# Another order of the head pairs in a hybrid decoder step: 1, 2, 3, 0 for the delta rule and 1, 0 for retention and GLA

## The chip, the cores and the metric

The kernel is one program on one core of a Trainium2 chip. The core has a matrix engine (TensorE, PE in the profile; its weight loads are PEld), a vector engine (VectorE, DVE), a scalar engine (ScalarE, ACT), GpSimd (POOL) and a queue engine, SyncE (SP), that issues most of the transfers between the chip's DRAM and its on-chip memory. The metric is the device time of one execution in microseconds (us); lower is better.

## The reference

One layer of a decoder is computed for 256 prompt tokens and for 8 x 4 sample tokens, 288 columns in all, which share the weights. The three mixers read the same normalised input, each through its own columns of one wide weight matrix, and their outputs are merged:

```python
h = rmsnorm(x, norm_mix)
(rq, rk, rv, rg, dqkv, da, db, dz, lq, lk, lv, llr, lgt, mg) = jnp.split(h @ w_in, IN_OFFSETS, axis=-1)
# branch 0: retention, 4 heads (dk 128, dv 256), gated by silu(rg)
# branch 1: gated delta rule, 8 heads (dk = dv = 128), conv of width 4 over q, k, v, gated by silu(dz)
# branch 2: GLA, 4 heads (dk 128, dv 256), a forget gate from llr, gated by silu(lgt)
br = jnp.einsum('blnc,ncd->blnd', jnp.stack([y_ret, y_gdn, y_gla], axis=2), w_branch)
gates = jax.nn.sigmoid(mg + b_merge).reshape(b, l, 3, D_MODEL)
x = x + jnp.sum(gates * br, axis=2) @ w_o
x = x + swiglu(rmsnorm(x, norm_ffn))      # w_gate_up, w_down
```

All numbers are float32, D_MODEL is 2048, and the width of the feed-forward part is 5632. Besides the two outputs y, the new recurrent states of all heads and the last rows before the convolution are written. The heads of a mixer do not depend on each other.

## The kernel before

The activations are held transposed, 16 blocks of 128 rows by 288 columns, each split into a high and a low part (`xh`, `xl`). A weight block goes through the same steps everywhere: SyncE loads it (`raw`, a ring of 4 buffers of 512 KB), ScalarE copies the high part (`wh`, lines 353, 384, 420), VectorE subtracts for the low part (`wl`, line 133), and TensorE does three matmuls, high by high, high by low, low by high (line 127).

The mixers work by pairs of heads: 4 pairs of the delta rule (`gdn`), 2 of retention (`ret`), 2 of GLA (`gla`). A pair's dense part is projections: a delta-rule pair takes four of 256 columns (`gdn_conv` for query, key and value, and `gated` for the gate dz), a pair of the other two takes two of 256 (query, key) and two of 512 (value, gate, in `two_heads`). Each projection of 256 columns is 4 loads of 512 KB, each of 512 columns 8.

The rest of a pair (scores, states, norms) is a generator that is started when its projections are done and is advanced a step at a time by `pump`, called between the matmuls of the projections that follow. So a pair's own work runs beside the projections of the pairs behind it. The order is written out in `run`: delta rule 0, retention 0, delta rule 1, retention 1, delta rule 2, GLA 0, delta rule 3, GLA 1. When all delta-rule generators have ended, `branch(0, 0)` starts, the projection of retention's output; the last GLA pair is advanced within it. Then come `branch(1, 1)` for the delta rule, `branch(2, 2)` for GLA, `merge_out` and `ffn`.

Three things pass from one stage to another through DRAM:

- `ys`, 3 x 8 blocks of 128 x 288: each head stores its output (`finish`, line 647; one block for a delta-rule head, block h for head h; two for the others, blocks 2h and 2h + 1), and `branch` loads the eight blocks of its mixer in the order 0 to 7 into two buffers `yr` (line 1317) and splits them into `yh` and `yl`;
- `fsum`, the running sums of GLA's forget gates for both pairs, stored by `gate_cols` (line 548) and loaded by `gla` (line 1299);
- small scratch of the delta rule's triangular solve, whose place does not depend on the pair.

The first pair has three things of its own. In `setup`, the loads of its query weights are issued ahead, in halves of 256 KB between the loads of the input (line 209), and their products are made while the input is still being prepared (`self.early`, line 255). In `gdn`, the small projections for decay, beta and GLA's low-rank gate (`gates`, lines 446 to 474) stand between its key and its value. In `run`, constants of the wide heads are loaded (`wide_setup`) ahead of the first retention pair.

Code that depends on a head's number takes a column of a constant (`gcol`, `elb`, `sel`, `ccols`, `qdec`, `c_decay`, conv weights), a slice of a state in DRAM, a decay factor as an immediate, and the parity `h % 2` for one of two buffers.

The order of instructions on each engine is set before the run by a planner (`TileContext` with `schedule_with_timeline_sim=True`): it takes them by their place in the program, with the loads and splits of weights at a higher priority, as their dependencies, buffers and engines come free in its own model, and puts in the semaphore waits.

Of the kernel before, what the change touches and what calls it, by code (L numbers as in the profile page):

```python
# [25 lines left out]
KT = D // P  # L26
# [5 lines left out]
CHUNK = 256  # L32
# [7 lines left out]
R1 = 4  # L40
R2 = 6
EV = 9

O_RQ, O_RK, O_RV, O_RG = 0, 512, 1024, 2048
O_GQ, O_GK, O_GV = 3072, 4096, 5120
# [50 lines left out]
def blocks(t):  # L96
    return [t[:, k] for k in range(t.shape[1])]


class Trunk:  # L100
# [74 lines left out]
    def setup(self):  # L175
        nc, tc = self.nc, self.tc
# [23 lines left out]
        for n in range(D // XC):  # L200
            cs = slice(n * XC, (n + 1) * XC)
            nc.sync.dma_start(out=xa[:, :, cs], in_=xv[:, :, cs])  # L202
            if n == 0:
                nc.sync.dma_start(out=xb, in_=self.i["x_sample"].rearrange("b t c -> (b t) c"))
            if n % 2 == 0:
                raw = self.t(self.wp, (P, 4, CHUNK), "raw", bufs=4)
                self.ahead.append(raw)
            ks = slice(2 * (n % 2), 2 * (n % 2) + 2)
            nc.sync.dma_start(out=raw[:, ks], in_=self.w_in(O_GQ)[:, 2 * n:2 * n + 2])
        xd = self.t(self.dr, (KT, P, T), "xT")  # L210
        self.xT = xd
        self.ys = self.t(self.dr, (3, 8, P, T), "ys")
# [21 lines left out]
        def prep():  # L234
            for n in range(D // XC):
                xr = self.t(x0, (P, 2, T), "xr", bufs=4)
                for q in range(2):
                    k = 2 * n + q
                    ks = slice(k * P, (k + 1) * P)
                    pt = self.ps()  # L240
                    for g, (t0, w) in enumerate(GROUPS):
                        self.tr(pt[:, t0:t0 + w], xa[:, g, ks] if g < 2 else xb[:, ks])
                    gc = self.g_mix[:, k:k + 1]
                    self.act(self.xh[:, k, :], pt[:, :T], AF.Copy, scale=gc)
                    self.stt(self.xl[:, k, :], pt[:, :T], gc, self.xh[:, k, :].bitcast(F32), ALU.mult, ALU.subtract)
                    (nc.vector.tensor_copy if q else nc.scalar.copy)(xr[:, q], pt[:, :T])
                nc.gpsimd.dma_start(out=xd[2 * n:2 * n + 2].rearrange("k p t -> p k t"), in_=xr)
                yield
            while True:
                yield  # L250

        steps = prep()
        for _ in range(2):
            next(steps)
        self.early = self.products(blocks(self.xh), blocks(self.xl), self.w_in(O_GQ), KT, False, steps, False)
        ra = self.t(x0, (112, P), "ra")
        rows(nc.gpsimd, "norm_ffn", ra[96:112])
        nc.gpsimd.dma_start(out=ra[0:96], in_=self.i["gdn_conv_w"][0].rearrange("w (b p) -> (w b) p", p=P))
# [293 lines left out]
    def gdn_conv(self, pair, part):  # L552
# [8 lines left out]
        smp = [cat[:, mm_, 3 + NPR:CW].rearrange("p (b r) -> p b r", r=7) for mm_ in range(2)]  # L561
        out = self.t(m, (P, 2, T), "ev", bufs=EV)

# [40 lines left out]
    def gated(self, n, c0):  # L604

        out = self.t(self.mx, (P, 2, T), "ev", bufs=EV)

# [9 lines left out]
    def two_heads(self, cv, cg, head, kind):  # L617

        vs = [self.t(self.mx, (P, 2, T), "ev", bufs=EV) for _ in range(2)]

# [5 lines left out]
        self.start(head(0, vs[0], gates), 1, kind)  # L626
        gs = [self.t(self.mx, (P, 2, T), "ev", bufs=EV) for _ in range(2)]

# [349 lines left out]
    def gdn(self, pair):  # L978
        q = self.gdn_conv(pair, 0)
        k = self.gdn_conv(pair, 1)  # L980
        if pair == 0:
            self.gates()
        v = self.gdn_conv(pair, 2)
        sz = self.gated(2, O_DZ + pair * CHUNK)
        self.start(self.gdn_mix(pair, q, k, v, sz), 1, "gdn")
# [111 lines left out]
    def evict_scaled(self, c0, perm=False):  # L1097
        out = self.t(self.mx, (P, 2, T), "ev", bufs=EV)

        def ev(m, pp):  # L1100
            self.tt(out[:, m], pp, self.rb, ALU.mult)

        self.x_in(c0, ev, perm)
        return out


    def rotated(self, c0):
        out = self.t(self.mx, (P, 2, T), "ev", bufs=EV)

        def ev(m, pp):  # L1110
            b = self.r1()
            self.tt(b[0:64], pp[64:128], self.rot[64:128, 1], ALU.mult)
            self.tt(b[64:128], pp[0:64], self.rot[0:64, 1], ALU.mult)
            self.tt(out[:, m], pp, self.rot[:, 0], ALU.mult)
            self.tt(out[:, m], out[:, m], b, ALU.add)

        self.x_in(c0, ev, perm=True)
        return out
# [350 lines left out]
    def run(self):  # L1469
        self.setup()  # L1470
        mst, gst, fst, bst = (ExitStack() for _ in range(4))
        dst = ExitStack()
        self.mx = self.pool("mixers", stack=mst, side="right")
        self.wd = self.pool("wide", stack=mst, side="right")
        self.gd = self.pool("gdn", stack=dst, side="right")
        self.gdn_setup()
        for f, pair in ((self.gdn, 0), (self.ret, 0), (self.gdn, 1), (self.ret, 1),
                        (self.gdn, 2), (self.gla, 0), (self.gdn, 3), (self.gla, 1)):
            if f == self.ret and pair == 0:
                self.wide_setup()  # L1480
            f(pair)
        while any(kind == "gdn" for _, _, kind in self.active):
            self.pump()
        dst.close()
        self.bp = self.pool("branch", stack=bst)
        self.branch(0, 0)
        while self.active:
            self.pump()
        mst.close()
        self.ap = self.pool("accum", side="right")  # L1490
        self.acc = self.accs()
        self.branch(1, 1)
        mp = self.pool("merged", stack=gst, side="right")
        mt = [self.t(mp, (P, KT, T), f"m{z}", F32R) for z in range(2)]
        merged = [(mt[0][:, k], mt[1][:, k]) for k in range(KT)]

        def emit(k, a):
            hi, lo = merged[k]
            self.act(hi, a, AF.Copy, scale=0.5)
            self.stt(lo, a, 0.5, hi.bitcast(F32), ALU.mult, ALU.subtract)  # L1500

        self.branch(2, 2, emit=emit)
        self.merge_out(merged, mp)
        gst.close()
        bst.close()
        self.actp = self.pool("act")
        self.ffn(fst)
        fst.close()
# [38 lines left out]
```

## Time and profile before

| | |
|---|---|
| timed runs, us | 2267.48, 2272.69, 2272.87 (median 2272.69) |
| profiled execution, us | 2270.85 |
| its span, first to last instruction, us | 2269.0 |
| mean granted TensorE clock | 0.978 of full speed |
| TensorE busy, us | 2178.8 (96%) |
| VectorE busy, us | 1356.2 (60%) |
| ScalarE busy, us | 1026.6 (45%) |
| GpSimd busy, us | 204.9 (9%) |
| read from DRAM, written to it | 342.02 MB, 26.92 MB |

The span is what the profile's rows divide up; the execution's own time is 1.85 us longer. Busy times are shares of that span. The granted clock is what the throttle gave TensorE, 1.00 being 2.4 GHz and 0.5 being 1.2 GHz; a stretch between the two has parts at either.

### The profile page before, as it was taken

The numbers are of one execution on the slowest core, as the hardware profiler recorded it, in microseconds if no ns is written. First come the engines' busy times: TensorE is split into PE (matmuls) and PEld (weight loads), VectorE is DVE, ScalarE is ACT, GpSimd is POOL, SyncE is SP. The second block draws the span as 40 slices with busy tenths as digits, with TensorE's granted clock in tenths as the row PEclk, the third lists the DMA queues.
The fourth block names the chain that finished last, engine by engine and source line by source line (L and its number), as shares of the span: only waits on it lengthen the run. The fifth ranks groups of instructions, "written<-read, shape, count | busy, mean of one in ns | idle before, by whom it ended". The sixth has DMA issues, their size and how long they took to land.

```text
span 2269.0 us, 42856 instructions
## 1 busy us (share of the span) xinstructions
PE 2178.8 (96%) x16476; PEld 2117.5 (93%) x16476; DVE 1356.2 (60%) x2940; ACT 1026.6 (45%) x2114; POOL 204.9 (9%) x264
## 2 busy tenths in 40 slices
PE   8699998998999999999999999999999999999997
PEld 7688898998898999999999999999999999999997
DVE  4465686686589577555556566555655445555554
ACT  4353553454355345444444455444444334444443
POOL 2000320232143124000000000000000000000000
PEclk8799999998999999999999999999999999999999
DMA  9876675587567555766666556655555555555553
GB/s 176 107 127 141 134 192 151 135 164 167 118 154 197 154 157 178 213 190 176 189 185 167 165 179 184 184 164 165 166 168 167 167 162 167 166 167 168 167 159 117
DMA packets 258456, 371.73 MB, mean 164 GB/s; under 512 B 26242, under 2 KB 126684, under 8 KB 258092
## 3 DMA queue, kind: packets, MB, share of 16 engines
q1 hardware_dynamic: 257084, 366.22, 61.6%
q8 instruction: 129, 2.11, 0.4%
q0 software_dynamic: 896, 2.45, 0.3%
q14 instruction: 75, 0.61, 0.1%
q10 hardware_dynamic: 272, 0.34, 0.1%
HBM read 342.02 MB, written 26.92 MB: 163 GB/s over the span
## 4 chain that ended last, share of the span: by engine, by line
PE 79%; DMA 11%; DVE 4%; ACT 2%; SPq 1%; issue 1%; POOL 1%; POOLq 0%; DVEq 0%; ACTq 0%
PE pd L127 48%; PE pm L127 30%; DMA raw<-in_w_in_dram 4%; DMA yr<-ys 2%; DVE wl L133 1%; DMA s<-in_state_ret_dram 1%; PE pm L124 1%; DMA srow<-in_state_gdn_conv_dram 1%; DMA out_dram<-s 1%; DMA dgu<-u 1%; DVE r L142 1%; DMA uc<-dgu 0%; DMA ys<-yo 0%; SPq L202 0%; ACT wh L420 0%
## 5 line engine op out<-in xcount | busy, mean ns | idle before, releaser
L133 DVE TENSOR_TENSOR wl<-raw,wh 128x512 fp32r<-128x512 f32 (+1 forms) x1208 | 847.8, 705 | 727.4 <-ACT wh L384 490.9
L127 PE MATMUL pd<-xh,wh 128*128 128x288 f32 x2768 | 831.3, 302 | 21.9 <-ACT wh L420 14.3
L127 PE MATMUL pd<-xl,wh 128*128 128x288 f32 x2768 | 832.0, 301 | 0.2 <-DVE xl L142 0.2
L127 PE MATMUL pd<-xh,wl 128*128 128x288 f32 x2768 | 824.4, 302 | 2.2 <-DVE wl L133 2.0
L384 ACT CAST wh<-raw 128x512 fp32r<-128x512 f32 x784 | 485.1, 620 | 644.6 <-PE pd L127 333.6
L127 PEld LDWEIGHTS pd<-xh,wh 128*128 128x128 f32 x2768 | 529.6, 192 | 29.3 <-ACT wh L420 15.8
L127 PEld LDWEIGHTS pd<-xh,wl 128*128 128x128 f32 x2768 | 527.0, 192 | 8.5 <-DVE wl L133 5.6
L127 PEld LDWEIGHTS pd<-xl,wh 128*128 128x128 f32 x2768 | 530.8, 192 | 3.9 <-issue 1.2
L353 ACT CAST wh<-raw 128x512 fp32r<-128x512 f32 x224 | 137.7, 619 | 206.0 <-PE pd L127 187.7
L127 PE MATMUL pm<-xh,wl 128*128 128x288 f32 x704 | 207.8, 295 | 0.0
L127 PE MATMUL pm<-xl,wh 128*128 128x288 f32 x704 | 207.3, 294 | 0.0
L127 PE MATMUL pm<-xh,wh 128*128 128x288 f32 x704 | 207.0, 294 | 0.0
L420 ACT CAST wh<-raw 128x512 fp32r<-128x512 f32 x192 | 117.3, 620 | 116.5 <-DMA raw<-in_w_in_dram 54.8
L127 PEld LDWEIGHTS pm<-xl,wh 128*128 128x128 f32 x704 | 132.1, 188 | 0.0
L127 PEld LDWEIGHTS pm<-xh,wh 128*128 128x128 f32 x704 | 132.1, 188 | 0.0
L127 PEld LDWEIGHTS pm<-xh,wl 128*128 128x128 f32 x704 | 132.0, 188 | 0.0
L127 PE MATMUL pd<-ah,wl 128*128 128x288 f32 x352 | 103.9, 295 | 0.0
L127 PE MATMUL pm<-ah,wl 128*128 128x288 f32 x352 | 103.9, 295 | 0.0
L127 PE MATMUL pm<-al,wh 128*128 128x288 f32 x352 | 103.8, 295 | 0.0
L127 PE MATMUL pd<-al,wh 128*128 128x288 f32 x352 | 103.7, 295 | 0.0
L127 PE MATMUL pm<-ah,wh 128*128 128x288 f32 x352 | 103.7, 295 | 0.0
L127 PE MATMUL pd<-ah,wh 128*128 128x288 f32 x352 | 103.6, 294 | 0.0
(368 smaller groups left out, 2892.0 us busy)
## 6 DMA issues: line engine op xcount, KB each, us to landing
raw<-in_w_in_dram SPq DMA_DIRECT2D x252, 512.0 KB
raw<-in_w_gate_up_dram SPq DMA_DIRECT2D x176, 512.0 KB
raw<-in_w_down_dram SPq DMA_DIRECT2D x88, 512.0 KB
raw<-in_w_branch_dram SPq DMA_DIRECT2D x48, 512.0 KB
raw<-in_w_o_dram SPq DMA_DIRECT2D x32, 512.0 KB
out_dram<-s SPq DMA_DIRECT2D x16, 512.0 KB
s<-in_state_gdn_dram SPq DMA_DIRECT2D x8, 512.0 KB
s<-in_state_ret_dram SPq DMA_DIRECT2D x16, 256.0 KB
```

Of the source, the lines that this page charges most:

```text
L124: self.nc.tensor.transpose(out, in_, self.ident[:k, :k])
L127: self.nc.tensor.matmul(out, lhsT=lhsT, rhs=rhs, start=start, stop=stop)
L133: self.nc.vector.tensor_tensor(out, a, b, op=op)
L142: self.nc.vector.scalar_tensor_tensor(out, a, s, b, op0=op0, op1=op1)
L353: nc.scalar.copy(wh, src)
L384: nc.scalar.copy(wh, raw[:, k])
L420: nc.scalar.copy(h, src)
```

## The change

The order of the pairs becomes a constant, `ORDER = (1, 2, 3, 0)`, for the delta rule, and 1, 0 for retention and for GLA. The kinds still alternate as before: delta rule 1, retention 1, delta rule 2, retention 0, delta rule 3, GLA 1, delta rule 0, GLA 0. What belongs to the first delta-rule pair (loads ahead, early products, the gates' place) follows the pair that is first.

```diff
+ORDER = (1, 2, 3, 0)
...
-            nc.sync.dma_start(out=raw[:, ks], in_=self.w_in(O_GQ)[:, 2 * n:2 * n + 2])
+            nc.sync.dma_start(out=raw[:, ks], in_=self.w_in(O_GQ + ORDER[0] * CHUNK)[:, 2 * n:2 * n + 2])
...
-        self.early = self.products(blocks(self.xh), blocks(self.xl), self.w_in(O_GQ), KT, False, steps, False)
+        self.early = self.products(blocks(self.xh), blocks(self.xl), self.w_in(O_GQ + ORDER[0] * CHUNK), KT, False, steps, False)
...
         k = self.gdn_conv(pair, 1)
-        if pair == 0:
+        if pair == ORDER[0]:
             self.gates()
...
-        for f, pair in ((self.gdn, 0), (self.ret, 0), (self.gdn, 1), (self.ret, 1),
-                        (self.gdn, 2), (self.gla, 0), (self.gdn, 3), (self.gla, 1)):
-            if f == self.ret and pair == 0:
+        for n, (f, pair) in enumerate(((self.ret, 1), (self.ret, 0), (self.gla, 1), (self.gla, 0))):
+            self.gdn(ORDER[n])
+            if n == 0:
                 self.wide_setup()
             f(pair)
```

## Rows read from the trace of the kernel before

**Rows 1.** The profile page, head and part 1: busy us, share, instructions.

```profile
span 2269.0 us, 42856 instructions
...
PE 2178.8 (96%) x16476; PEld 2117.5 (93%) x16476; DVE 1356.2 (60%) x2940; ACT 1026.6 (45%) x2114; POOL 204.9 (9%) x264
```

**Rows 2.** The profile page, part 4: the chain that ended last, by engine.

```profile
PE 79%; DMA 11%; DVE 4%; ACT 2%; SPq 1%; issue 1%; POOL 1%; POOLq 0%; DVEq 0%; ACTq 0%
```

**Rows 3.** Busy time by stretch: from:to, length, busy us by engine, clock, DMA share.

```profile
core 0: us, PE busy (x) PEld busy (x) DVE busy (x) ACT busy (x) POOL busy (x), PEclk, DMA share, GB/s
0.00:151.00 151.00, 116.11 (x651) 105.22 (x652) 74.46 (x220) 65.06 (x160) 19.80 (x33) 0.82 0.89 137
...
219.00:352.00 133.00, 119.27 (x862) 109.83 (x861) 90.99 (x244) 66.89 (x178) 37.61 (x41) 0.96 0.68 156
...
410.00:539.00 129.00, 119.83 (x840) 110.43 (x839) 91.47 (x241) 64.13 (x179) 42.69 (x45) 0.96 0.75 162
...
605.00:725.00 120.00, 117.25 (x873) 108.35 (x872) 97.36 (x261) 65.11 (x176) 44.60 (x58) 1.00 0.67 155
...
990.00:2269.00 1279.00, 1261.17 (x9509) 1258.61 (x9507) 704.98 (x1238) 564.70 (x992) 1.70 (x2) 1.00 0.58 169
```

**Rows 4.** Waits in the first 151 us: engine line waited for: us, times, longest.

```profile
ACT wh L420 <- DMA raw<-in_w_in_dram: 48.7, 16, 5.2
...
ACT wh L171 <- DMA raw<-in_w_in_dram: 16.9, 4, 10.2
```

**Rows 5.** SyncE's queue, 175 to 182 us: start, length, line, what is issued.

```profile
179.58 1.78 SPq L548 DMA_DIRECT2D fsum<-ev  x2
```

**Rows 6.** SyncE's queue, 505 to 530 us.

```profile
507.46 4.74 SPq L647 DMA_DIRECT2D ys<-yo  x2
...
527.02 0.50 SPq L1299 DMA_DIRECT2D ev<-fsum  x1
```

**Rows 7.** SyncE's queue, 830 to 870 us.

```profile
838.95 0.34 SPq L1317 DMA_DIRECT2D yr<-ys  x1
839.38 0.38 SPq L647 DMA_DIRECT2D ys<-yo  x1
...
840.33 0.40 SPq L647 DMA_DIRECT2D ys<-yo  x1
...
856.95 1.88 SPq L1317 DMA_DIRECT2D yr<-ys  x2
```

**Rows 8.** SyncE's queue, 900 to 1180 us.

```profile
906.32 0.81 SPq L647 DMA_DIRECT2D ys<-yo  x2
...
988.21 0.34 SPq L1317 DMA_DIRECT2D yr<-ys  x1
...
989.58 0.46 SPq L1317 DMA_DIRECT2D yr<-ys  x1
...
1157.13 0.80 SPq L1317 DMA_DIRECT2D yr<-ys  x2
```

**Rows 9.** DMA issues of the whole run: what, queue, count, KB each.

```profile
s<-in_state_gdn_dram SPq DMA_DIRECT2D x8, 512.0 KB
s<-in_state_ret_dram SPq DMA_DIRECT2D x16, 256.0 KB
...
srow<-in_state_gdn_conv_dram SPq DMA_DIRECT2D x12, 24.0 KB
```

**Rows 10.** Busy time by stretch: projections of delta-rule pairs 1, 2, 3.

```profile
219.00:296.00 77.00, 71.57 (x526) 65.70 (x525) 49.27 (x135) 36.42 (x93) 19.95 (x25) 0.98 0.64 143
410.00:480.00 70.00, 68.23 (x498) 62.81 (x497) 50.63 (x135) 33.98 (x90) 23.45 (x25) 1.00 0.66 156
605.00:661.00 56.00, 56.00 (x426) 51.88 (x425) 41.14 (x132) 26.79 (x73) 16.51 (x27) 1.00 0.66 151
```

**Rows 11.** The chain that ended last, 270 to 300 us: start, us, what.

```profile
277.67 8.84 DMA ys<-yo
```

**Rows 12.** The chain that ended last, 980 to 1010 us.

```profile
989.58 5.13 DMA yr<-ys
```

## The prediction

> **What bounds the kernel now.** I read the page first. TensorE is busy 96% of the span and no other engine passes 60% [rows 1]; the chain of work that ended last is 79% TensorE and 11% waits for DMA [rows 2]. So a change moves the time only if it changes how much TensorE has to do, or lengthens or shortens the stretches in which TensorE is short of work. Next I cut the span at the places where the loads change from the delta-rule kind to the wide-head kind [rows 3]. From 990 us on there are only 17.83 us without TensorE work in 1279 (1279.00 - 1261.17), and the granted clock is 1.00, the level of 2.4 GHz: that is the branch projections, the merge and the feed-forward part, and the change does not enter it except through what the mixers left in DRAM. In the mixers, up to 990 us, the missing work is larger: 34.89 us in the first 151 us, 13.73 in the second delta-rule stretch, 9.17 in the third, 2.75 in the fourth. If the change does anything, it does it there. I then asked what the opening waits for [rows 4]: ScalarE, which makes the high part of each weight block, waited 48.7 us for the 512 KB weight loads and 16.9 us for the small gate loads. Last I followed SyncE's queue of issues to the places where one pair's result in DRAM is read by a later stage [rows 5 to 8].
>
> **The change part by part.** *What it removes and adds.* No operation is removed or added. The kinds of work still come in the order delta rule, retention, delta rule, retention, delta rule, GLA, delta rule, GLA; the gate projection still stands behind the first pair's key convolution, and the setup of the wide heads behind the first delta-rule pair. Only the pair number handed to each place differs. Every pair issues the same things: 16 loads of 512 KB for its four projections (4 in 256 KB halves for whichever pair is first), three loads of old conv rows, two of recurrent state, and so on; the counts of the whole run are those of four equal pairs, for instance 12 loads of conv rows, 8 of delta-rule state, 16 of retention state [rows 9]. A head's parity within its pair, which picks between two buffers, is unchanged. So TensorE, VectorE, ScalarE and GpSimd get the same instructions with the same shapes, at other columns of the constants: 0 us.
>
> *What moves in the queues.* In SyncE's queue nothing is moved past anything: the 64 delta-rule weight loads, the 48 of retention and the 48 of GLA keep their places and sizes, and only the DRAM address of each differs, by a multiple of 1 KB in every weight row for the delta rule. The loads whose waiting costs something are those of the opening. Is pair 1's slice fetched at another rate than pair 0's? No row shows pair 0 and pair 1 in the same place, so I bound it by the delta-rule projections of pairs 1, 2 and 3 [rows 10]: GB/s over the busy share of the DMA engines gives 143/0.64 = 223, 156/0.66 = 236 and 151/0.66 = 229. The extremes lie 6% apart, with other traffic beside them. If the whole 48.7 us of waiting scaled by that 6%, the opening would move by 2.9 us, up or down. Nearest to the case is the middle one, 229, which is 3% from either end and has no sign, so I take 0 and keep -2.9 and +2.9. The 16.9 us for the gates concern columns that every order reads first: 0. The clock in the opening is 0.82 [rows 3], between the two levels of 1.2 and 2.4 GHz, in both orders, because the same waits are there; 0.
>
> *What is read in another order.* Three results pass through DRAM. The forget sums of both GLA pairs are stored together at 179.58 us [rows 5], and the first of them is fetched at 527.02 [rows 6]; pair 1's sums, now the first wanted, have 347 us of slack. Retention's last blocks are stored from 507.46 us [rows 6] and the first branch starts to read its blocks at 838.95 [rows 7]: that its first-read blocks 0 to 3 are now the last written uses none of the 326 us after those. GLA's last blocks are stored at 906.32 and first read at 1157.13 [rows 8], 250 us. The tightest is the delta rule. The last pair's two blocks are stored at 839.38 and 840.33 [rows 7]; before they were blocks 6 and 7, and the second branch reads those last; now they are blocks 0 and 1, which it reads first, at 988.21 and 989.58 [rows 8]. From 839.38 to 988.21 are 148.8 us, so the wait is 0. What hides it is the first branch, which lies between with TensorE busy; if that cover were gone, a load right behind its store would wait for it. Nearest rows for that price: from 277.67 us the chain follows a block's store for 8.84 us until it has landed [rows 11], and a load of a block at 989.58 takes 5.13 us to land [rows 12], together 14.0 us. Bounds: 0 and +14.0; I take 0, because 148.8 is ten times that.
>
> The Trainium skill, "DMA: Bandwidth & Descriptors", section "Two DMAs through the same engine are not ordered", says that a DMA which reads what an earlier one writes must wait for that one's completion, whatever queue both are on; by that rule the new reading order is the one thing here that could cost, and the same page (section "Anatomy of one DMA") puts the fixed part at about 2 us, by which an uncovered wait would make 2273.8 us and not the 2285.8 below. The trace has the store and its reader 148.8 us apart, so rule and rows both leave nothing to pay.
>
> *The sum.* The profiled execution took 2270.85 us (span 2269.0 and 1.85 around it); 2270.85 + 0 + 0 + 0 = 2270.85. The median of the three timed runs is 1.84 higher, 2272.69, and they lie between 2267.48 and 2272.87. With a change of nothing the best guess is between profiled run and median: (2270.85 + 2272.69) / 2 = 2271.8 us.
>
> **The rivals.** *Hand-over, slower.* The planner that orders each engine's instructions could fetch the second branch's blocks as soon as the two "yr" buffers are free, about 859 us, when the first branch has issued its last [rows 7]. Then its first load would wait for the newest store, and behind it in SyncE's queue stand the weight loads, which ScalarE and TensorE want. For it: the blocks first read are the newest. Against it: the queue left those buffers alone from 859 to 988 us, and 859 is still 18 us after the stores. It decides only if the load comes within 8.84 us of the store. Price 14.0: 2285.8 us.
>
> *Another plan.* Instruction order comes from a planner, and other addresses could give it another dependency or price. For it: like stretches did not run alike. The three that hold one delta-rule pair and the next wide pair's queries and keys took 133, 129 and 120 us [rows 3]. If the first two came out like the third, 13 + 9 = 22 us would go: 2249.8. If the last two came out like the first, 4 + 13 = 17 would be added: 2288.8. Against it: the three differ in what runs beside them (retention's heads in the first two, GLA's in the third), which the change keeps in place, and sizes and dependencies are the same one for one.
>
> *Load rate.* Pair 1's columns come 6% faster or slower than pair 0's did: 2268.9 or 2274.7. To pass 0.3%, which is 6.8 us and about what a measurement of this kernel can tell from no change, the 48.7 us of waiting would have to change by 14%, more than twice what the three pairs show.
>
> **How the numbers follow.** No change 0.88; load rate 0.03, which also stays within 0.3%; another plan 0.07, of which 0.04 to the fast side and 0.03 to the slow; hand-over 0.02. Hence faster by over 0.3% 0.04, within 0.91, slower 0.03 + 0.02 = 0.05. The time is that of no change, 2271.8. The range takes the spread of the three runs and the 2.9 us of the loads on either side: 2267.48 - 2.9 = 2264.6 and 2272.87 + 2.9 = 2275.8, rounded outwards to 2264 and 2276. The first two cases lie in it, 0.91; the others need not be.
>
> **What would show it.** If right: the same count of instructions and the same bytes in each queue; the stretches of [rows 3] within 2 or 3 us of their lengths; the waits of the opening for weights within 2.9 us of 48.7; the last delta-rule blocks stored near 840 us and the second branch's first load near 988, with no wait for a store in front of it. If "yr" loads appear before 900 us, or ScalarE waits for them much longer, it was the hand-over. If one mixer stretch is longer or shorter by 5 us or more with the same instructions in another order, it was the plan. If the opening alone is longer and its waits for weight loads with it, it was the load rate. The prediction is wrong if the sequence of instructions on an engine changes for a reason that no row shows.

## The result: faster by 1%

The changed kernel takes 2246.97 us (median of four runs, 2246.63 to 2249.73) against 2271.08 us (median of four, 2267.48 to 2272.87): a ratio of 0.9899, 95% interval 0.9883 to 0.9914. The forecast was no change, 2271.8 us with a range of 2264 to 2276. The time lies 17 us below the range.

**The profile after.** First the head and the busy time of the page.

```profile
span 2244.8 us, 42856 instructions
...
PE 2166.5 (97%) x16476; PEld 2108.7 (94%) x16476; DVE 1354.1 (60%) x2940; ACT 1026.3 (46%) x2114; POOL 207.0 (9%) x264
```

The counts of instructions are those of [rows 1]. I also laid the two traces' lists of instructions side by side, engine by engine and without the rows of the semaphore waits: the kind and the order are the same on every engine, save for a few memsets of VectorE that are recorded a place or a few earlier or later. The same work is done in the same sequence and 24.2 us of the span are gone (2269.0 - 2244.8).

Next, busy time by stretch: from:to, length, busy us by engine, granted clock, DMA share, GB/s.

```profile
0.00:107.00 107.00, 96.44 (x651) 89.24 (x652) 74.03 (x221) 65.39 (x160) 20.22 (x33) 0.95 0.81 194
...
490.00:550.00 60.00, 58.93 (x562) 56.77 (x562) 38.52 (x108) 23.48 (x50) 6.57 (x10) 0.97 0.50 148
550.00:605.00 55.00, 52.77 (x391) 48.54 (x390) 36.01 (x112) 23.57 (x63) 13.81 (x24) 0.97 0.80 114
605.00:650.00 45.00, 40.67 (x295) 37.12 (x293) 36.88 (x97) 23.00 (x57) 15.88 (x21) 1.00 0.96 125
650.00:696.00 46.00, 33.54 (x199) 30.14 (x198) 24.18 (x53) 18.36 (x57) 14.85 (x14) 0.78 0.74 148
```

The first line answers to the first of [rows 3]: the same 651 matmuls that took 151 us take 107. Time without TensorE work falls from 34.89 to 10.56 us (107 - 96.44), and the work itself from 116.11 to 96.44, with a granted clock of 0.95 in place of 0.82: TensorE stands still less, and more of the stretch is at the level of 2.4 GHz. (Busy time times clock is nearly the same in both: 116.11 x 0.82 = 95.2 and 96.44 x 0.95 = 91.6 us.) The DMA engines move 194 GB/s at a share of 0.81 in place of 137 at 0.89. Then look at 550 to 696 us, where pair 0 now stands: at 605 to 650 us the engines are busy for 0.96 of the time and move only 125 GB/s, and from 650 to 696 TensorE works for 33.54 of 46 us at a clock of 0.78. The low rate has moved with pair 0.

Now SyncE's queue. Line 346 loads the first weights of each wide pair's value projection, and so marks where a delta-rule pair's place ends; lines 1318 and 648 are the reads and stores of `ys`.

```profile
106.91 0.37 SPq L346 DMA_DIRECT2D raw<-in_w_in_dram  x1
...
306.80 0.37 SPq L346 DMA_DIRECT2D raw<-in_w_in_dram  x1
...
490.25 0.37 SPq L346 DMA_DIRECT2D raw<-in_w_in_dram  x1
...
696.19 0.38 SPq L346 DMA_DIRECT2D raw<-in_w_in_dram  x1
...
814.09 0.34 SPq L1318 DMA_DIRECT2D yr<-ys  x1
814.52 0.38 SPq L648 DMA_DIRECT2D ys<-yo  x1
...
815.47 0.40 SPq L648 DMA_DIRECT2D ys<-yo  x1
...
832.19 1.85 SPq L1318 DMA_DIRECT2D yr<-ys  x2
...
963.41 0.34 SPq L1318 DMA_DIRECT2D yr<-ys  x1
```

The same marks in the kernel before, where the line is 345:

```profile
151.23 0.37 SPq L345 DMA_DIRECT2D raw<-in_w_in_dram  x1
...
351.99 9.74 SPq L345 DMA_DIRECT2D raw<-in_w_in_dram  x4
...
538.57 9.87 SPq L345 DMA_DIRECT2D raw<-in_w_in_dram  x4
...
725.05 0.38 SPq L345 DMA_DIRECT2D raw<-in_w_in_dram  x1
```

They cut both spans into five pieces:

| piece | before, us | after, us | difference |
|---|---|---|---|
| opening: setup, first delta-rule pair, the first wide pair's queries and keys | 151.2 | 106.9 | -44.3 |
| second place | 200.8 | 199.9 | -0.9 |
| third place | 186.6 | 183.5 | -3.1 |
| fourth place (pair 3 before, pair 0 after) | 186.5 | 205.9 | +19.4 |
| the rest, to the end | 1543.9 | 1548.6 | +4.7 |
| sum | 2269.0 | 2244.8 | -24.2 |

So the change gains 44 us at the start and pays back 24 later. From the first read of `ys` to the end both kernels take the same (2269.0 - 838.95 = 1430.1 us before, 2244.8 - 814.09 = 1430.7 after), so the 4.7 us of the last piece lie before the first branch. Last, the waits: engine and line, what for, us in total, times, longest. The first two lines are of 0 to 107 us and answer to [rows 4]; the third is of 550 to 696 us.

```profile
ACT wh L421 <- DMA raw<-in_w_in_dram: 17.9, 10, 4.4
...
ACT wh L172 <- DMA raw<-in_w_in_dram: 6.1, 1, 6.1
...
ACT wh L421 <- DMA raw<-in_w_in_dram: 21.4, 7, 5.1
```

ScalarE's wait for weight loads in the opening falls from 48.7 to 17.9 us, its wait for the small gate loads from 16.9 to 6.1, and 21.4 us of the same wait appear where pair 0 went. Loads of the same size, in the same place of the same queue, arrive faster when they are pair 1's.

### The profile page after: what moved, and what is told of

Read it like the earlier page. It is cut to its first block, busy times and chain, and to the rows that moved or that the text cites. A ratio compares the mean times of both kernels' runs of the same rounds, so it can differ in the third digit from the quotient of the medians.

```text
span 2244.8 us, 42856 instructions
## 1 busy us (share of the span) xinstructions
PE 2166.5 (97%) x16476; PEld 2108.7 (94%) x16476; DVE 1354.1 (60%) x2940; ACT 1026.3 (46%) x2114; POOL 207.0 (9%) x264
## 4 chain that ended last, share of the span: by engine, by line
PE 81%; DMA 11%; DVE 4%; SPq 1%; ACT 1%; issue 1%; POOL 0%; POOLq 0%; DVEq 0%; ACTq 0%
PE pd L128 49%; PE pm L128 31%; DMA raw<-in_w_in_dram 5%; DMA yr<-ys 1%; DVE wl L134 1%; PE pm L125 1%; DMA s<-in_state_ret_dram 1%; DMA out_dram<-s 1%; DMA dgu<-u 1%; DMA uc<-dgu 1%; DMA xa<-in_x_prompt_dram 0%; DMA srow<-in_state_gdn_conv_dram 0%; DMA b<-dgbs 0%; DVE ev L143 0%; DVE s L143 0%
```

## The experiments

**Theory A: the address.** The rate of a weight load depends on the columns it reads, and pair 0's are slow. Pair 0's slices of query, key, value and gate begin at bytes 12288, 16384, 20480 and 24640 of each row of `w_in`: three are multiples of 4096, the last is 64 bytes past one. Pairs 1, 2 and 3 lie 1024, 2048 and 3072 bytes further on. **Theory B: the order.** Which heads come first, with their states, constants and blocks of `ys`, makes the time.

**Addresses and order apart.** Three kernels use a map from pair to weight columns. The first is the kernel before with only the columns permuted; the second is the changed kernel with the columns put back in the old sequence; the third is the kernel before with pair 0 reading pair 1's columns, 1 KB further on.

```diff
+COL = (1, 2, 3, 0)   # second kernel: (3, 0, 1, 2) with ORDER kept; third: (1, 1, 2, 3)
+WCOL = (1, 0)        # second: (1, 0); third: (0, 1)
...
-        self.x_in(O_GQ + c0, ev)
+        self.x_in(O_GQ + part * 1024 + COL[pair] * CHUNK, ev)
...
-        sz = self.gated(2, O_DZ + pair * CHUNK)
+        sz = self.gated(2, O_DZ + COL[pair] * CHUNK)
...
-        q = self.rotated(O_RQ + pair * CHUNK)
+        q = self.rotated(O_RQ + WCOL[pair] * CHUNK)
```

> The kernel before, with its heads in the order 0, 1, 2, 3, but each pair's projections read the weight columns that the changed kernel reads in that place (delta rule 1, 2, 3, 0; retention and GLA 1, 0); so heads are computed from other heads' projection weights, and states, outputs and constants stay in the old order. Theory A (where a weight load's columns begin in DRAM sets its rate; loads of pair 0 are slow): the whole gain comes along, about 2247 us, with the first delta-rule stretch some 44 us shorter and the place of the fourth longer. Theory B (the order of states, outputs and hand-over blocks makes the difference): about 2271 us, as before.

> The changed kernel, with its heads in the order 1, 2, 3, 0, but each place reads the weight columns that the kernel before reads there (0, 1, 2, 3 and 0, 1); again heads get other heads' projection weights. Theory A: the gain is gone, about 2271 us. Theory B: the gain stays, about 2247 us.

> The kernel before, with one thing changed: the 16 weight loads of delta-rule pair 0 read the columns of pair 1 (1 KB further in each row), so pair 0 is computed from pair 1's weights. Theory A: the opening gains its 44 us and no later delta-rule stretch gives any back, so faster than the changed kernel: about 2230 us. Theory B: 2271 us.

| kernel | us | ratio to before | 95% |
|---|---|---|---|
| only the weight columns moved | 2244.79 | 0.9886 | 0.9868 to 0.9903 |
| everything but the weight columns moved | 2271.13 | 1.0006 | 0.9995 to 1.0017 |
| old order, pair 0 reads pair 1's columns | 2226.64 | 0.9814 | 0.9793 to 0.9835 |

The columns alone give the whole gain, and the order of heads without them gives nothing: theory B falls. In the kernel with the heads moved, the first 151 us are those of the kernel before again:

```profile
0.00:151.00 151.00, 116.64 (x659) 104.73 (x660) 75.20 (x225) 65.67 (x161) 19.79 (x33) 0.84 0.87 138
```

In the third kernel no delta-rule projection reads a slow slice, and ScalarE's wait in the opening (0 to 105 us) is short again:

```profile
ACT wh L422 <- DMA raw<-in_w_in_dram: 11.3, 8, 4.0
```

This kernel also prices the slow slices by place: against its 2226.6 us they cost 43 us first (2269.6, the kernel before on the same chip), and about 20 us last (2246.97, the changed kernel, timed in another session; by the two ratios to the kernel before, 0.9899 and 0.9814, it is 19).

**Which part of the change.** Two kernels apply one half of it each: the delta rule's order alone (retention and GLA 0, 1), and the order of retention and GLA alone (delta rule 0, 1, 2, 3).

> One part of the change alone: delta-rule pairs in the order 1, 2, 3, 0, retention and GLA in the old order 0, 1. Theory A (rate set by the columns): nearly all of the gain is the delta rule's, whose rows of 1 KB load slowest against the TensorE time that they feed: 2243 to 2252 us. If the wide heads' part carries the gain: 2265 us or more.

> The other part alone: delta-rule pairs in the old order 0, 1, 2, 3, retention and GLA in the order 1, 0. Theory A: the slow first pair stays in the opening, so 2266 to 2275 us. If the wide heads' part carries the gain: about 2250 us.

The delta rule alone: 2245.9 us, ratio 0.9887 (0.9867 to 0.9906). Retention and GLA alone: 2271.78 us, ratio 1.0012 (0.9999 to 1.0024). The gain is the delta rule's. That was not given by the loads alone: by the load kernels below, retention's pair 0 and GLA's pair 0 have slow query slices too (bytes 0 and 28736, 96 and 94 us, against 65 and 58 for their pairs 1), yet moving those changed nothing that could be measured.

**The load rate by itself.** A kernel that only loads: 16 loads of 512 KB in groups, four in flight; the first column is moved by some bytes from group to group, and a small sum on VectorE marks when a group has landed. A slice with rows of 1 KB is 2.1 MB, so a group reads it four times over. It computes nothing of the reference, and it ran once, as did the three load kernels that follow; the slice of pair 0's query was timed in two of the four, at 97 and 96 us.

```diff
+for gi, (how, kn, w, off) in enumerate(GROUPS):
+    v = src.rearrange("(k p) c -> p k c", p=P)[:, :, 3072 + off // 4:3072 + off // 4 + w]
+    for n in range(16):
+        raw = wp.tile([P, kn, w], F32, tag="raw", bufs=4)
+        nc.sync.dma_start(out=raw, in_=v[:, n * kn % 16:n * kn % 16 + kn])
```

> No computation of the reference, only weight loads: 20 groups of 16 loads of 512 KB, four in flight, each group from other columns of the input weights. Groups 1 to 13 read rows of 1 KB at 0, 64, 128, 256, 512, 1024, 1536, 2048, 2560, 3072, 3584, 3840 and 4096 bytes behind the first byte of pair 0's query columns, which is a multiple of 4096 bytes into the row; groups 14 to 17 rows of 2 KB at 0, 1024, 2048, 3072; groups 18 to 20 rows of 1 KB at 0, 1024, 2048, but with partition p holding 16 neighbouring rows in place of every 128th. Theory A: at 0 and 4096 about 130 GB/s or less, at 1024 to 3072 above 200, with small offsets still slow; by its mechanism (16 engines reading in step land in the same 4 KB blocks) the other row assignment shows no dependence on the offset. If all groups run alike within 5%, the address alone does not slow a load and A falls.

VectorE's timeline gives the marks (start in us first); the time of a group is the difference of two marks that follow each other, and of the first group the time from the first load at 1.07 us.

```profile
97.72 0.16 DVE L38 TENSOR_TENSOR mark<-a,b 128x1 f32<-128x1 f32 x1
...
393.23 0.16 DVE L38 TENSOR_TENSOR mark<-a,b 128x1 f32<-128x1 f32 x1
...
449.99 0.16 DVE L38 TENSOR_TENSOR mark<-a,b 128x1 f32<-128x1 f32 x1
...
849.08 0.16 DVE L38 TENSOR_TENSOR mark<-a,b 128x1 f32<-128x1 f32 x1
...
945.77 0.16 DVE L38 TENSOR_TENSOR mark<-a,b 128x1 f32<-128x1 f32 x1
```

| bytes past 12288 | 0 | 64 | 128 | 256 | 512 | 1024 | 1536 | 2048 | 2560 | 3072 | 3584 | 3840 | 4096 |
|---|---|---|---|---|---|---|---|---|---|---|---|---|---|
| us for 8.39 MB, 1 KB a row | 97 | 93 | 82 | 62 | 59 | 57 | 50 | 52 | 50 | 55 | 91 | 101 | 97 |

The group of pair 0's query (0) takes 97 us, 87 GB/s; pair 1's (1024, marks 393.23 to 449.99) 57 us, 148 GB/s. It begins again after 4096 bytes (849.08 to 945.77, 97 us). With 2 KB a row, as for the wide value and gate projections, 0, 1024, 2048 and 3072 took 49, 29, 29 and 52 us: good and bad places again, at about half the level, but here 3072 is a bad one (such a row reaches 1024 bytes past the next multiple of 4096). The step from the bad columns to the good is as expected; the level of the good is not, since more than 200 GB/s had been expected and 148 to 168 came. I had also expected the slowness to come from the row that each partition gets, with 16 engines in step. In that form it fell: with 16 neighbouring rows in each partition 0, 1024 and 2048 gave 108, 63 and 58 us, the same dependence.

**Other matrices.** The same kernel on `w_gate_up` (rows 45056 bytes apart) and `w_branch` (8192 bytes apart), on a slow and a fast slice of `w_in` in turn, and on the other mixers' columns of `w_in`, whose rows are 65664 bytes apart.

> Loads alone again, no computation of the reference: groups of 16 loads of 512 KB, four in flight. Groups 1 to 6: the gate and up weights (rows 45056 bytes apart, 11 times 4096) in pieces of 1 KB at 0, 512, 1024, 2048, 3072, 3584; groups 7 to 9: the branch weights (rows 8192 apart) at 0, 1024, 2048; group 10: the input weights, loads of a slow and a fast slice in turn (bytes 12288 and 14336); groups 11 to 13: its rows of 2 KB at 4096, 41088 and 43136; groups 14 to 19: 1 KB at 0, 1024, 24640, 25664, 28736, 29760. Theory A1 (a piece that lies badly within 4 KB is slow in any matrix): groups 1 and 6 take 80 us or more, as the slow slices of the input weights did, and groups 3 and 4 some 50. Theory A2 (the input weights' rows, 128 bytes over a multiple of 65536 apart, fall on few memory channels for some columns): groups 1 to 9 do not depend on the offset in that way. Both: 14, 16, 18 slow (80 us or more), 15, 17, 19 fast (below 65); group 10 near the mean of slow and fast, 73, if a slow load holds up the queue behind it, and near 50 if the two overlap.

```profile
27.52 0.16 DVE L39 TENSOR_TENSOR mark<-a,b 128x1 f32<-128x1 f32 x1
...
54.95 0.16 DVE L39 TENSOR_TENSOR mark<-a,b 128x1 f32<-128x1 f32 x1
...
245.08 0.16 DVE L39 TENSOR_TENSOR mark<-a,b 128x1 f32<-128x1 f32 x1
...
297.01 0.16 DVE L39 TENSOR_TENSOR mark<-a,b 128x1 f32<-128x1 f32 x1
```

`w_gate_up` took 26.5 to 27.4 us at each of six offsets and `w_branch` about 27 at each of three: 308 GB/s, with no bad place. So of these three matrices the place within 4096 bytes matters in `w_in` alone, where with rows of 1 KB even the good places are half as fast. There it matters in every region tried: 1 KB rows at 0 took 96 us and at 1024 took 65; 24640 and 25664 took 93 and 62, 28736 and 29760 took 94 and 58; 2 KB rows at 4096, 41088 and 43136 took 50, 46 and 30. A slow and a fast slice in turn took 51.9 us (245.08 to 297.01), less than the mean of the two alone, (97 + 52) / 2 = 74: these slow loads did not hold up the fast ones beside them.

**The distance between rows.** Slices of `w_in` are copied into three matrices in DRAM whose rows are 65664, 69632 and 66688 bytes apart, and loaded from there at eight offsets.

> Loads alone, no computation of the reference: the same columns of the input weights are first copied within DRAM into three scratch matrices of 2048 rows, with rows 65664, 69632 and 66688 bytes apart, and then loaded from each in 8 groups of 16 loads of 512 KB, rows of 1 KB, at 0, 512, 1024, 1536, 2048, 2560, 3072 and 3584 bytes. If the distance between the rows is the cause, the first matrix has a slow stretch of offsets (80 us or more a group) and none below 45 us, and the second, a multiple of 4096 as the gate and up weights are, takes about 27 us at all of them; the third, 1024 bytes over 65664, is not fixed by anything measured, and anything but a stretch as slow as the first's speaks for the distance. If the place of the input weights in memory is the cause, all three scratch matrices take the same.

```profile
544.18 0.16 DVE L42 TENSOR_TENSOR mark<-a,b 128x1 f32<-128x1 f32 x1
...
612.61 0.16 DVE L42 TENSOR_TENSOR mark<-a,b 128x1 f32<-128x1 f32 x1
...
640.29 0.16 DVE L42 TENSOR_TENSOR mark<-a,b 128x1 f32<-128x1 f32 x1
...
833.96 0.16 DVE L42 TENSOR_TENSOR mark<-a,b 128x1 f32<-128x1 f32 x1
861.15 0.16 DVE L42 TENSOR_TENSOR mark<-a,b 128x1 f32<-128x1 f32 x1
```

The same columns took 40 to 68 us at 65664 bytes, and 27 to 28 us at every offset at 69632 and at 66688. So the distance between rows decides whether a slice can be slow, and the first column decides only within a bad distance. Two misses lie in it: at least 80 us had been expected at the bad places of the copy at 65664, and the slowest group that can be read took 68.4 (offset 3584; 544.18 to 612.61); and none below 45 us, but offsets 1536 and 2560 took 40 and 42. The group at offset 0 ran together with the copying and is not read, and the copy lies at another address than `w_in`. Whether that is why it is milder stays open: the address of the whole matrix was not varied by itself.

The Trainium skill, "DMA: Bandwidth & Descriptors", section "Latency and other measured facts", has a rule on this: copies slow down where the distance between partitions' rows is a large power of two, 4 KiB more restores the rate and 192 bytes more does not; the cause it gives, streams in step that fall on the same memory channel, it marks as an inference. Its copies go from DRAM to DRAM, with distances of 512 KiB and more and rows of 16 KiB, so these runs lie outside what it measured. They look alike: 65664 is 64 KiB and 128 bytes and is slow, 69632 is 64 KiB and 4 KiB and is fast. They add that 64 KiB and 1152 bytes is enough, that 8192 bytes, a smaller power of two, is fast, and that in a slow matrix the first column makes a factor of two. The cause isn't shown here either.

**Which slow slices get in each other's way.** Pair 0's four slices alone and in turn.

> Loads alone, no computation of the reference, 16 loads of 512 KB a group, four in flight, from the input weights. Groups 1 to 4: the slices of pair 0's query, key, value and gate (bytes 12288, 16384, 20480, 24640), each by itself; groups 5 to 10: query and key, query and value, value and gate, key and gate, query and pair 1's query in turn, and all four in turn; groups 11 to 13: rows of 2 KB at 4096, at 8192, and the two in turn. If each slow slice crowds a few memory channels and different slices crowd different ones, groups 1 to 4 take 85 to 100 us and groups 5 to 8 and 10 take 50 to 65. If all slow slices crowd the same ones, groups 5 to 8 and 10 take 85 to 100 as well, and only group 9 some 55 to 75.

```profile
97.50 0.16 DVE L37 TENSOR_TENSOR mark<-a,b 128x1 f32<-128x1 f32 x1
...
385.93 0.16 DVE L37 TENSOR_TENSOR mark<-a,b 128x1 f32<-128x1 f32 x1
...
439.20 0.16 DVE L37 TENSOR_TENSOR mark<-a,b 128x1 f32<-128x1 f32 x1
...
536.08 0.16 DVE L37 TENSOR_TENSOR mark<-a,b 128x1 f32<-128x1 f32 x1
```

Alone, query, key, value and gate took 96.4, 97.9, 97.0 and 93.5 us. Query and key in turn took 53.3 (385.93 to 439.20) for the same number of bytes, value and gate 53.6, all four in turn 53.9; query and value in turn took 96.9 (439.20 to 536.08), key and gate 94.9. Neither expectation came whole. In the pairs tried, slices whose 4096-byte blocks are neighbours overlap, and those two blocks apart share one limit. Query and pair 1's query in turn took 51.9; rows of 2 KB at 4096 and at 8192 took 49.3 and 48.7, and in turn 29.8.

**Other places for pair 0.** If the 24 us paid back late could be avoided, a version near the 2226.6 us of the third kernel would be had. Seven kernels look for it; one of them is a control.

The first puts pair 0 third: `ORDER = (1, 2, 0, 3)`.

> The changed kernel with delta-rule pair 0 third and not last: order 1, 2, 0, 3. Theory A: the 16 slow loads cost about 20 us wherever the matrix engine has other pairs' work beside them, so 2243 to 2252 us, and the long stretch moves from the fourth place to the third. A rival by which it is the first place that is bad for pair 0 alone, whatever is slow: the third place as short as before, about 2227 us.

It took 2257.1 us, 0.9941 (0.9926 to 0.9955). The long place moved to third as expected, 201.7 us against 183.5, but the opening and the fourth place were also longer than in the changed kernel (110.5 against 106.9, and 192.0 against the 186.5 of pair 3 before), so the sum misses the expectation by 5 us. Against the third kernel's 2226.6 us the slow slices cost about 30 us here, not the 20 of the last place: other pairs' work beside them does not give one price. The stretch with pair 0's projections in this kernel:

```profile
410.00:511.00 101.00, 83.42 (x546) 77.57 (x543) 57.45 (x158) 43.83 (x120) 26.52 (x30) 0.88 0.89 165
```

The next three put the wide pair's query projection behind pair 0's query and its key projection behind pair 0's key, so that loads of both kinds alternate, though four at a time and not one by one as in the load kernel: last place in the changed order, third place, and last place with retention and GLA in the old order.

```diff
-    def gdn(self, pair):
+    def gdn(self, pair, wide=None, wpair=0):
+        steps = wide(wpair, True) if wide else iter(())
...
+        next(steps, None)
...
+            if n == 3:
+                self.gdn(ORDER[n], f, pair)
+                continue
```

> The changed kernel with the projections of its last place taken in turn: pair 0's query, GLA's query, pair 0's key, GLA's key, pair 0's value and gate, then GLA's value and gate, so that slow and fast loads are in flight together. Theory A: the loads overlap as they did when issued in turn by themselves, and up to 19 us of the last place come back: 2228 to 2240 us. Rival (a slow load holds the queue whatever lies beside it, or the later start of pair 0's own steps is paid at the end): 2245 us or more.

> The same taking in turn with pair 0 third (order 1, 2, 0, 3), beside the first GLA pair. Theory A: 2230 to 2245 us, at least 10 us under the kernel with pair 0 third and not taken in turn, 2257 us. Rival: no faster than that one.

> As the first of these, with retention and GLA in the order 0, 1, so that the last place holds GLA's pair 1, whose rows of 2 KB load fast. Theory A: a little below the first, by up to 5 us: 2224 to 2238 us. Rival: 2245 us or more.

They took 2257.99 us (0.9951, 0.9934 to 0.9968), 2254.08 (0.9937, 0.9914 to 0.9960) and 2255.4 (0.9949, 0.9928 to 0.9969): misses of 18, 9 and 17 us, all on the rivals' side. The first was no clean test, since the query slice of its GLA pair (byte 28736) is itself a slow one; the other two have GLA's pair 1, whose query slice (29760) is fast, and gained no more that could be measured. In the first of them the place is as long as in the changed kernel (485.02 to 692.01 us, 207 against 205.9), pair 0's own steps begin later, and TensorE runs short behind it:

```profile
692.00:735.00 43.00, 35.02 (x234) 32.72 (x234) 24.94 (x80) 20.95 (x64) 8.12 (x12) 0.85 0.69 169
```

The first branch's first load came at 840.3 us in place of 814.1.

The last three use what the slices in turn had shown: a pair is projected two projections at a time, query with key and value with gate, with the loads taken in turn.

```diff
+    def both(self, a, eva, b, evb):
+        for k0 in range(0, KT, 4):
+            raws = [self.load(self.w_in(c)[:, k0:k0 + 4], 4) for c in (a, b)]
...
+        if pair in FUSED:
+            self.both(O_GQ + a[0], a[1], O_GQ + b[0], b[1])
```

One has pair 0 so in the last place, one in the second place (`ORDER = (1, 0, 2, 3)`), and the control has pair 3 so, whose loads are not slow.

> The changed kernel with pair 0, still last, projected two at a time: query and key, then value and gate, with the loads of the two in turn. If different slices crowd different channels: most of the 19 us of the last place come back, 2226 to 2238 us. If the slow slices share one bottleneck: 2243 to 2252 us, no gain.

> The same with pair 0 second (order 1, 0, 2, 3). Different channels: 2226 to 2242 us; one bottleneck: 2245 us or more.

> The control: the changed kernel with pair 3, whose slices load fast, projected two at a time in its place, and pair 0 as in the change. Either theory of the loads: no gain, 2242 to 2254 us; if two at a time helps by itself, it shows here as well, 2238 us or less.

They took 2254.06 us (0.9921, 0.9899 to 0.9942), 2251.03 (0.9910, 0.9896 to 0.9925) and, the control, 2248.1 (0.9900, 0.9883 to 0.9916), alike with the changed kernel as expected. The other two were misses of 16 and 9 us. In the one with pair 0 last, two views over its place, waits and stretches:

```profile
ACT wh L569 <- PE pd L129: 12.8, 15, 2.3
PEld pm L129 <- issue: 12.4, 12, 9.4
ACT ns L638 <- DMA out_dram<-ns: 12.1, 1, 12.1
```

```profile
650.00:693.00 43.00, 26.87 (x174) 25.40 (x173) 24.03 (x47) 13.17 (x33) 9.77 (x10) 0.82 0.79 144
```

ScalarE's wait for weight loads there falls from 21.4 to 5.5 us, which fits loads that overlap in the kernel as they did alone. But two convolutions now end together and share the one buffer `ns` (12.1 us), and TensorE works for 26.87 of 43 us where the changed kernel has 33.54 of 46. The place itself is 4 us shorter than in the changed kernel (491.37 to 693.09, 201.7 against 205.9), the opening 3 us longer (110.0), and all that stands behind the place 10 us longer (1558.7 against 1548.6). So the loss lies mostly behind the place; what makes it was not isolated. No version that computes the reference was measurably faster than the changed kernel.

## Why the prediction was wrong

**What bounds the kernel: right.** It said that a change moves the time only through the stretches in which TensorE is short, and named the opening as the largest with 34.89 us. That is where the 44.3 us came from, and from the first read of `ys` on nothing changed (1430.1 and 1430.7 us), as it said of the part behind the mixers.

**No work added, sequence kept: right.** Counts and order agree on every engine, so the rival of another plan was false. Half of its sign came out, mixer stretches that move by 5 us or more, but not the other half, another order. That its price to the fast side, 2249.8 us, lies 3 us from the measured time is a coincidence: it took 13 and 9 us from the second and third delta-rule stretch, and the time came out of the opening.

**Hand-over of `ys`: right at nothing, for a wrong reason.** The slack was misread. The prediction took the load at 988.21 us for the second branch's first [rows 8] and counted 148.8 us from the store. But `branch` reads eight blocks, and ten reads of `ys` stand in the queue of the kernel before between 838.95 and 856.95 us, those of [rows 7] and

```profile
839.82 0.42 SPq L1317 DMA_DIRECT2D yr<-ys  x1
...
842.21 1.76 SPq L1317 DMA_DIRECT2D yr<-ys  x2
...
847.15 8.61 SPq L1317 DMA_DIRECT2D yr<-ys  x4
```

So the pair at 856.95 [rows 7] are already the second branch's blocks 0 and 1, fetched into the two `yr` buffers as soon as they were free. The rival held that this could happen, and the argument against it, that the queue left those buffers alone, was false. Its sign, reads of `ys` before 900 us, shows nothing, as they stand there in both kernels. In the changed kernel the newest blocks are stored at 814.52 and 815.47 us and fetched at 832.19, 17.7 us after the first store. The wait is still 0: the fetch stands where it stood (18.10 us after the first read of `ys`, and 18.00 before) and takes 1.85 us in the queue as against 1.88. The margin over the 8.84 us of [rows 11] is 9 us and not 140. The section of the Trainium skill from which the prediction takes its 2 us measures transfers that GpSimd issues; the stores and reads of `ys` are SyncE's, and no run here shows an uncovered wait.

**The load rate: the step that failed.** "Is pair 1's slice fetched at another rate than pair 0's? No row shows pair 0 and pair 1 in the same place, so I bound it by the delta-rule projections of pairs 1, 2 and 3." The bound was 6%, 2.9 us. It compared the three pairs that turned out to be alike (57, 52 and 55 us alone) and never pair 0 (97 us). The step took for a spread of all pairs what was a spread among the others, and gave the rival 0.03. Its mechanism was the true one; its size was 44.3 us in the opening, fifteen times the bound.

A row for pair 0 was there. The ratio used for the three, GB/s over DMA share, gives 137 / 0.89 = 154 for the opening of before [rows 3], against 223 to 236 in [rows 10]. I had not formed it, though it is where pair 0's loads are. The opening has other small loads, which might have been blamed; but they are the same after the change, and there the ratio is 194 / 0.81 = 240. Also, 48.7 us of waiting was read as if it could only shrink in proportion to a small difference in rate; it fell by 30.8. And the 16.9 us for the gates were put at nothing because every order reads those columns; they fell by 10.8, with the same columns. These loads stand behind pair 0's in the queue; whether that held them up was not tested by itself. The two waits together fell by 41.6 us, which goes with the 44.3 of the opening.

**The clock: wrong with it.** "0.82 in both orders, because the same waits are there; 0." The waits were not the same. Of the 44 us, 24.3 are time without TensorE work (34.89 - 10.56) and 19.7 are the same 651 matmuls done in less time (116.11 - 96.44), at 0.95.

**What no step had.** The slow loads were not removed but moved: of the 44.3 us gained, 19.4 came back in the last place and 4.7 behind it. From 490 to 696 us TensorE works for 185.9 us (58.93 + 52.77 + 40.67 + 33.54) and is idle for 20.1; in the like place of before it works for 180.3 of 187:

```profile
538.00:725.00 187.00, 180.32 (x1443) 168.38 (x1443) 136.97 (x369) 89.84 (x229) 51.19 (x68) 0.98 0.64 147
```

The last place has more than twice the opening's matmuls (1447 against 651) to lie over the slow loads, which goes with the lower price; that this is the whole reason was not tested alone.

The sign given for the load rate came out in the main: the opening and its waits for weights changed together, with the sequence kept. It had said the opening alone, and the last place changed as well.

## What to carry to other kernels

Before you call an edit of addresses free, form bytes per second over DMA share for each stretch that reads a slice, above all the one that the edit moves, and do not bound an unmeasured slice by the others. Time the loads of a matrix for several first columns with nothing else running: rows 65664 bytes apart, 128 over 64 KiB, had good and bad columns, and rows 8192, 45056, 66688 and 69632 bytes apart had none. 1 KB more between rows, or another first column, was worth a factor of about two here. Where a slow load stands matters: the same slow slices cost 43 us in the opening, where TensorE had little else to do, about 30 in the third place and about 20 in the last.

## What the runs showed of the hardware

- 8.39 MB in loads of 512 KB with rows of 1 KB took 26.5 to 28.1 us from rows 45056, 8192, 69632 or 66688 bytes apart at every first column tried; from rows 65664 bytes apart it took 50 to 101 us in `w_in`, every 128th row to a partition, and 40 to 68 in a copy.
- In `w_in` the first column decides: 97 us from 12288, 57 us from 1024 bytes further on, 97 again 4096 bytes further on; rows of 2 KB took 49 and 29 us at the first two.
- Two slow slices taken in turn took 53 to 54 us where they lie in neighbouring blocks of 4096 bytes, and 95 to 97 where they lie two blocks apart (two pairs each). Which part of the memory this is can't be told from these runs.
